# Strassen products for the merge gates and half of the branch gates of a two-layer encoder

## The chip, the cores and the metric

The kernel runs on one core of a Trainium2 chip. The metric is the device time of one execution in microseconds (us); below 0.2% (3.5 us) a difference can hardly be told from none.

## The reference, cut to what matters

```python
# x: (512, 1024) fp32, two layers, each:
h = rmsnorm(x, g_norm)
u = h @ w_in                       # one combined projection, all branches and gates
# A: 8 heads of differential attention -> o_a (rmsnorm over 128), B: dilated attention -> o_b,
# M: attention to 256 memory tokens -> o_m
y_a = (o_a * silu(dg)) @ w_br_diff     # dg, lg, mg: columns of u, 1024 + 512 + 512 wide
y_b = (o_b * silu(lg)) @ w_br_dil
y_m = (o_m * silu(mg)) @ w_br_mem
gates = sigmoid(mgate)                 # 3 x 1024 columns of u
merged = gates[0] * y_a + gates[1] * y_b + gates[2] * y_m
x = x + merged @ w_out
# end: rmsnorm(x, g_final)
```

## The kernel before, in words

The normalised input of a layer stands transposed in SBUF, as hT (128 x 8 x 512: eight k-slices of 128 channels, 512 tokens). Every fp32 operand is held as two parts: `split` (L95, L96) rounds a tile to its hi part on ScalarE (ACT) and subtracts that on VectorE (DVE) for the lo part, and `mm3` (L167 to L169) makes each product from three matmuls: hi by hi, hi by lo, lo by hi. A projection of 128 output channels (`proj_fm`) is so 8 x 3 = 24 matmuls on TensorE (PE) of 128x128 weights against 128x512 of hT. Weights come by DMA through `prefetch` (L141) two blocks ahead, in the order that `weight_order` writes out: 512 KB to `w_raw`, then `split` to `w_hi` and `w_lo` (128x1024 each).

A layer first does memory attention, then four rounds of differential and dilated attention. Work that PE can do at any time is woven with work that waits for softmaxes: `weave` takes turns between two generators. The last dilated attention, `dil_att(l, 3)`, has no partner. `diff_norm` makes the mean square of each head for the rmsnorm over 128 (`f_ms`), adds eps on ACT (`f_sq`, L446), takes the reciprocal on DVE (L447), and stores it to DRAM as `v_d`; the attention outputs go to DRAM as `u_d`. After this comes `merge`:

- 16 branch gates: `gate` makes x * sigmoid(x) of one projection; `u_raw` (a head's output, read back from `u_d`) is multiplied by it (L592), for the first eight also by the root of `v_d` (L589), and split to `u_hi`, `u_lo`, which stay in SBUF.
- For each of eight d (128 output channels): three merge gates (projections from hT, sigmoid), then the products `ya`, `yb`, `ym_ps` of the kept U with the branch weights, and their gated sum, split to `mg_hi`, `mg_lo`.

`out_proj` then multiplies these by `w_out`. The order of the instructions on each engine is set when the kernel is built, by a scheduler that runs a timeline of its own; on the chip each engine then takes its list in order.

Of the kernel before, what the change touches and what calls it, by code (L numbers as in the profile page):

```python
# [44 lines left out]
def encoder_kernel(ctx: ExitStack, tc: tile.TileContext, x, mem, g_norm, w_in, diff_lambda,  # L45
# [100 lines left out]
    ready = []  # L146

    def prefetch(n):
        while len(ready) < n and order:
            key, k, cols, pieces = order.pop(0)  # L150
            raw = wp.tile([128, k, cols], F32, tag="raw", name="w_raw", bufs=3)
            for k0, k1, c0, c1, src in pieces:
                dma(raw[:, k0:k1, c0:c1], src.rearrange("(k p) n -> p k n", p=128))
            hi = wp.tile([128, k, cols], F32R, tag="hi", name="w_hi", bufs=4)
            lo = wp.tile([128, k, cols], F32R, tag="lo", name="w_lo", bufs=3)
# [15 lines left out]
    def proj_fm(l, col):  # L171

        hi, lo = weight("in", l, col)
        o = mm([128, S])
# [4 lines left out]
    def gate(l, col):
# [397 lines left out]
        spill(o, 8 + h, P)  # L577


    def merge(l, yu, ym, lam_init):  # L580
        U = {}
        for i in U_ORDER:
            raw = yu.tile([128, S], F32, tag="ul", name="u_raw", bufs=3)
            dma(raw, u_d[i])
            if i < 8:
                v = yu.tile([128, S], F32, tag="uv", name="u_v", bufs=3)
# [10 lines left out]
        M = []  # L597
        for d in range(8):
            gs = []
            for b in range(3):  # L600
                o = proj_fm(l, MGATE + b * 1024 + d * 128)
                g = sg_tile(name="mgate")
                nc.scalar.activation(g, o, AF.Sigmoid)
                gs.append(g)
            whi, wlo = weight("ba", l, d)
            ya = mm([128, S])
            for k in range(8):
                mm3(ya, whi[:, k], wlo[:, k], U[k][0], U[k][1], k == 0, k == 7)
            whi, wlo = weight("bm", l, d)
            ym_ps = mm([128, S])  # L610
            yb = mm([128, S])
            for k in range(8):
                mm3(ym_ps if k < 4 else yb, whi[:, k], wlo[:, k], U[8 + k][0], U[8 + k][1], k % 4 == 0, k % 4 == 3)
            for g, y in zip(gs, (ya, yb, ym_ps)):
                nc.vector.tensor_tensor(out=g, in0=y, in1=g, op=ALU.mult)  # L615
            nc.vector.tensor_tensor(out=gs[0], in0=gs[0], in1=gs[1], op=ALU.add)
            nc.vector.tensor_tensor(out=gs[0], in0=gs[0], in1=gs[2], op=ALU.add)
            hi = ym.tile([128, S], F32R, tag="mg", name="mg_hi", bufs=16)
            lo = ym.tile([128, S], F32R, tag="mg", name="mg_lo", bufs=16)
            split(hi, lo, gs[0])  # L620
            M.append((hi, lo))
# [203 lines left out]
```

## Time and profile before

| | before |
|---|---|
| time, median of 3 runs | 1770.03 us (1769.4 to 1770.7) |
| the profiled execution: its time, its span | 1770.44 us, 1768.4 us |
| granted TensorE clock, mean | 0.998 |
| PE busy | 1743.8 us, 99% |
| DVE busy | 1005.5 us, 57% |
| ACT busy | 834.5 us, 47% |
| POOL (GpSimd) busy | 22.1 us, 1% |
| branch gates, first layer | about 540 to 637 us |
| merge gates and branch products, first layer | about 640 to 848 us |
| the same two in the second layer | about 1408 to 1505 us, 1505 to 1716 us |

A share is of the span, over stages with different limits. PE's busy time counts pipelined matmuls that overlap (a 128x512 matmul is shown with 0.39 us, but the next one starts 0.23 us after it), so the pitch, the distance from start to start, is what a matmul costs.

### The profile page before, as it was taken

How to read it: one execution, taken by the hardware profiler on the slowest of the kernel's cores; microseconds unless marked ns; L12 is line 12 of the kernel's file. 1: busy time of each engine (PE TensorE's matmuls, PEld its weight loads, DVE VectorE, ACT ScalarE, POOL GpSimd, SP SyncE). 2: the span in 40 equal slices, each digit the busy share in tenths (PEclk: the TensorE clock that was granted, in tenths of full speed). 3: DMA queues.
4: the chain of work that ended last, by engine and by line, in shares of the span. 5: the costliest groups of instructions: out<-in, count | busy, mean ns of one | idle time of the engine just before them, and what ended most of it. 6: DMA issues, size and time to landing. Idle time of an engine off the chain costs nothing.

```text
span 1768.4 us, 23429 instructions
## 1 busy us (share of the span) xinstructions
PE 1743.8 (99%) x9012; PEld 1496.0 (85%) x9012; DVE 1005.5 (57%) x1727; ACT 834.5 (47%) x1436; POOL 22.1 (1%) x45
## 2 busy tenths in 40 slices
PE   7999999999999999999999999999999999999998
PEld 6798889888888888888888898888988888888886
DVE  6566576666765663333465656658566747333333
ACT  6455555545555642222255555455454548322223
POOL 2200000000000000000000000000000000000000
PEclk9999999999999999999999999999999999999999
DMA  9643243332432643333572333324332336333342
GB/s 263 141 130 86 72 123 89 103 94 76 117 97 80 202 138 95 97 93 116 160 199 59 112 85 103 94 76 116 95 98 86 101 109 202 107 96 95 96 154 72
DMA packets 308847, 200.26 MB, mean 113 GB/s; under 512 B 14116, under 2 KB 283428, under 8 KB 308736
## 3 DMA queue, kind: packets, MB, share of 16 engines
q1 hardware_dynamic: 306704, 195.09, 38.3%
q0 software_dynamic: 2032, 3.68, 1.2%
q8 instruction: 71, 1.16, 0.3%
q14 instruction: 40, 0.33, 0.1%
HBM read 177.89 MB, written 20.83 MB: 112 GB/s over the span
## 4 chain that ended last, share of the span: by engine, by line
PE 97%; DMA 1%; ACT 1%; DVE 0%; issue 0%; SPq 0%; DVEq 0%; ACTq 0%
PE mm L167 27%; PE mm L169 27%; PE mm L168 27%; PE wT_ps L384 2%; PE f_s L407 2%; PE f_s L408 2%; DMA w_raw<-in_w_mem_kv 1%; PE f_o L168 1%; PE f_o L169 1%; PE f_o L167 1%; PE d_o L533 1%; PE d_s L509 1%; PE w_ps L522 0%; PE d_o L168 0%; PE d_o L169 0%; PE d_o L167 0%
## 5 line engine op out<-in xcount | busy, mean ns | idle before, releaser
L96 DVE TENSOR_TENSOR w_lo<-w_raw,w_hi 128x1024 fp32r<-128x1024 f32 (+2 forms) x296 | 335.8, 1135 | 436.1 <-PE mm L169 389.7
L95 ACT ACTIVATE w_hi<-w_raw 128x1024 fp32r<-128x1024 f32 (+2 forms) x296 | 293.3, 991 | 601.5 <-PE mm L168 296.0
L167 PE MATMUL mm<-hT_hi,w_hi 128*128 128x512 f32 x1344 | 529.9, 395 | 1.9 <-ACT hT_hi L95 1.9
L169 PE MATMUL mm<-hT_hi,w_lo 128*128 128x512 f32 x1344 | 527.3, 392 | 0.0
L168 PE MATMUL mm<-hT_lo,w_hi 128*128 128x512 f32 x1344 | 526.7, 392 | 0.0
L167 PEld LDWEIGHTS mm<-hT_hi,w_hi 128*128 128x128 f32 x1344 | 252.8, 188 | 53.2 <-ACT hT_hi L95 2.1
L169 PEld LDWEIGHTS mm<-hT_hi,w_lo 128*128 128x128 f32 x1344 | 252.9, 188 | 53.0 <-DVE w_lo L96 0.4
L168 PEld LDWEIGHTS mm<-hT_lo,w_hi 128*128 128x128 f32 x1344 | 253.0, 188 | 50.7
L169 PE MATMUL mm<-w_hi,hT_lo 128*128 128x384 f32 (+1 forms) x512 | 160.8, 315 | 0.0
L167 PE MATMUL mm<-w_hi,hT_hi 128*128 128x384 f32 (+1 forms) x512 | 160.0, 313 | 0.0
L168 PE MATMUL mm<-w_lo,hT_hi 128*128 128x384 f32 (+1 forms) x512 | 158.5, 310 | 0.0
L413 ACT ACTIVATE f_e<-f_e,f_st 128x512 f32<-128x512 f32 x128 | 91.9, 721 | 49.7 <-DVE f_st L410 49.7
L167 PE MATMUL mm<-u_hi,w_hi 128*128 128x512 f32 x256 | 101.2, 395 | 0.0
L169 PE MATMUL mm<-u_hi,w_lo 128*128 128x512 f32 x256 | 101.2, 395 | 0.0
L168 PE MATMUL mm<-u_lo,w_hi 128*128 128x512 f32 x256 | 101.1, 395 | 0.0
L167 PEld LDWEIGHTS mm<-w_hi,hT_hi 128*128 128x128 f32 x512 | 96.9, 189 | 1.0
L168 PEld LDWEIGHTS mm<-w_lo,hT_hi 128*128 128x128 f32 x512 | 96.8, 189 | 1.1
L169 PEld LDWEIGHTS mm<-w_hi,hT_lo 128*128 128x128 f32 x512 | 96.7, 189 | 0.0
L410 DVE CUSTOM_DVE_ANT_0 f_e<-f_s,f_bias 128x512 f32<-128x512 f32 x128 | 84.4, 681 | 6.8 <-PE f_s L408 6.7
L96 DVE TENSOR_TENSOR f_wTlo<-wT_ps,f_wThi 128x512 fp32r<-128x512 f32 x64 | 43.7, 683 | 31.4 <-ACT f_wThi L95 30.2
L615 DVE TENSOR_TENSOR mgate<-mm,mgate 128x512 f32<-128x512 f32 x48 | 33.0, 688 | 48.4 <-PE mm L169 48.4
L447 DVE RECIPROCAL f_sq<-f_sq 128x512 f32<-128x512 f32 x16 | 53.6, 3349 | 9.5 <-ACT f_sq L446 9.5
(203 smaller groups left out, 2403.9 us busy)
## 6 DMA issues: line engine op xcount, KB each, us to landing
w_raw<-in_w_in SPq DMA_DIRECT2D x168, 512.0 KB, 3.8
w_raw<-in_w_in SPq DMA_DIRECT2D x96, 128.0 KB, 2.4
w_raw<-in_w_mem_kv SPq DMA_DIRECT2D x16, 512.0 KB, 6.0
w_raw<-in_w_in SPq DMA_DIRECT2D x32, 256.0 KB, 2.9
u_raw<-u_d SPq DMA_DIRECT2D x32, 256.0 KB, 4.1
w_raw<-in_w_br_diff SPq DMA_DIRECT2D x16, 512.0 KB, 3.8
w_raw<-in_w_out SPq DMA_DIRECT2D x16, 512.0 KB, 3.9
f_bias<-tt_d SPq DMA_DIRECT2D x64, 112.0 KB, 4.1
```

The costliest lines, as they stand in the source:

```text
L95: nc.scalar.activation(hi, src, AF.Copy)
L96: nc.vector.tensor_tensor(out=lo, in0=src, in1=f32(hi), op=ALU.subtract)
L167: nc.tensor.matmul(o, lhsT=lh, rhs=rh, start=start, stop=False)
L168: nc.tensor.matmul(o, lhsT=lh, rhs=rl, start=False, stop=False)
L169: nc.tensor.matmul(o, lhsT=ll, rhs=rh, start=False, stop=stop)
L384: nc.tensor.transpose(t[:, i], s, ident)
L407: nc.tensor.matmul(sp, lhsT=qh[:, cs], rhs=K[s, m], start=True, stop=False)
L408: nc.tensor.matmul(sp, lhsT=ql[:, cs], rhs=K[s, m], start=False, stop=True)
L410: nc.vector.tensor_tensor_reduce(out=em.rearrange("p (c b) -> p c b", c=4), in0=sp, in1=bt[:, 3 - c:7 - c], op0=ALU.add, op1=ALU.min, scal ...
L413: nc.scalar.activation(em, em, AF.Exp, scale=-1.0, bias=stt[:, m:m + 1], accum_out=stt[:, 2 + m:3 + m])
L447: nc.vector.reciprocal(sq, sq)
L615: nc.vector.tensor_tensor(out=g, in0=y, in1=g, op=ALU.mult)
```

## The change

A pair of projections (two blocks of 128 columns) is one product of a 256x1024 weight block with the 1024x512 of hT. `pair` makes it by Strassen's scheme in Winograd's form: halves of the columns, of k and of the tokens, seven products instead of eight. Each product is 4 k-slices x 3 matmuls of 128x256. There are four branch pairs a layer (`U_PAIRS`, gates 4 to 7 and 12 to 15) and twelve merge pairs (`merge_steps`); eight branch gates stay single, and five of them (`gate_fill`) are now woven with `dil_att(l, 3)`. `load_pair` fetches the four quarters of a pair's weights (256 KB each) and makes the sums of quarters that the scheme needs with four GpSimd (POOL) operations; the sums are then split like other weights, in 3.5 units of 128x1024. `right_sums` makes the sums of hT's quarters once a layer: eight POOL additions of hi and lo (`b_q`), eight DVE subtractions, and eight splits into T0 to T3. Where a gate was one sigmoid and one multiply from PSUM, a pair is put together in SBUF by one ACT copy and eight DVE instructions of 128x256. The gated sums `m` are kept in fp32 (`m` tiles), and split into the place of hT after the last merge pair.

```diff
-U_ORDER = (8, 9, 10, 11, 0, 1, 2, 3, 4, 5, 12, 13, 14, 6, 7, 15)
+N_EARLY = 5
+U_ORDER = (8, 9, 10, 11, 0, 1, 2, 3)
+U_PAIRS = ((4, 12), (5, 13), (6, 14), (7, 15))
+def merge_steps(d0):
+    d1 = d0 + 1
+    return (("pair", (d0, 0), (d0, 1)), ("pair", (d0, 2), (d1, 2)), ("y", d0), ("pair", (d1, 0), (d1, 1)), ("y", d1))
...
+    def load_pair(key):
+        l, cols = key[1], key[2:]
+        pool = pair_pool[0]
+        t1, t2, t3 = [pool.tile([128, 8, 128], F32, tag="raw", name="s_raw", bufs=4) if i < 2 else
+                      wp.tile([128, 8, 128], F32, tag="raw", name="s_raw3", bufs=3) for i in range(3)]
+        t4 = pool.tile([128, 4, 128], F32, tag="raw4", name="s_raw4", bufs=2)
+        lo, up = slice(0, 4), slice(4, 8)
+        for t, part, f, k in ((t2, lo, 1, 0), (t3, up, 1, 1), (t1, lo, 0, 0), (t3, lo, 0, 1)):
+            src = w_in[l, k * 512:(k + 1) * 512, cols[f]:cols[f] + 128]
+            dma(t[:, part], src.rearrange("(k p) n -> p k n", p=128))
+        a11, a21, a12, a22 = t1[:, lo], t2[:, lo], t3[:, lo], t3[:, up]
+        tt = nc.gpsimd.tensor_tensor
+        tt(out=t2[:, up], in0=a21, in1=a22, op=ALU.add)
+        tt(out=t1[:, up], in0=t2[:, up], in1=a11, op=ALU.subtract)
+        tt(out=a21, in0=a11, in1=a21, op=ALU.subtract)
+        tt(out=t4, in0=a12, in1=t1[:, up], op=ALU.subtract)
...
+    def pair(l, colA, colB, B, gA, gB):
+        (b11, b21, b22), T = B
...
+        def prod(u, part, rhs):
...
+            o = mm([128, S], name="s_mm")[:, 0:256]
+            for k in range(4):
+                kk = 4 * part + k
+                mm3(o, hi[:, kk], lo[:, kk], rh[:, k], rl[:, k], k == 0, k == 3)
+            return o
...
+        nc.scalar.activation(c11, prod(0, 0, b11), AF.Copy)
+        add(c12, prod(0, 1, T[1]), c11)
+        add(c21, prod(1, 0, T[2]), c12)
+        o = prod(1, 1, T[0])
+        add(c22, o, c21)
+        add(c12, o, c12)
+        add(c11, prod(2, 0, b21), c11)
+        add(c21, prod(2, 1, T[3]), c21)
+        add(c12, prod(3, 0, b22), c12)
...
+    def right_sums(pool):
...
+                    b = pool.tile([128, 2, 256], F32, tag="uT", name="b_q", bufs=32)
+                    nc.gpsimd.tensor_tensor(out=b, in0=f32(hT_hi[:, ks, ts]), in1=f32(hT_lo[:, ks, ts]), op=ALU.add)
+                    q[kh, th] = b
...
+            sub(q[0, 0], q[0, 1], q[0, 0])
+            sub(q[0, 1], q[1, 1], q[0, 1])
+            sub(q[1, 1], q[1, 1], q[0, 0])
+            sub(q[1, 0], q[1, 0], q[1, 1])
+            ks = slice(2 * k2, 2 * k2 + 2)
+            for (hi, lo), b in zip(T, (q[0, 0], q[1, 1], q[0, 1], q[1, 0])):
+                split(hi[:, ks], lo[:, ks], b)
...
+        B = right_sums(yu)
+        for i in U_ORDER:
+            raw = load_u(i)
+            keep_u(i, raw, early[i] if i in early else gate(l, U_COLS[i]))
+        for two in U_PAIRS:
+            raws = [load_u(i) for i in two]
+            gs = [sg_tile(name="gate") for _ in two]
+            pair(l, *[U_COLS[i] for i in two], B, *gs)
+            for i, raw, g in zip(two, raws, gs):
+                sig = sg_tile(name="gate_s")
+                nc.scalar.activation(sig, g, AF.Sigmoid)
+                nc.gpsimd.tensor_tensor(out=raw, in0=raw, in1=g, op=ALU.mult)
+                keep_u(i, raw, sig)
...
+                    if step[1:] == LAST_PAIR:
+                        for e, m in enumerate(M):
+                            split(hT_hi[:, e], hT_lo[:, e], m)
...
-                weave((dil_att(l, j, P, dp), 4))
+                early = {}
+                def gate_fill():
+                    for i in U_ORDER[:N_EARLY]:
+                        early[i] = gate(l, U_COLS[i])
+                        yield
+                weave((gate_fill(), N_EARLY), (dil_att(l, j, P, dp), 4))
```

Places in the built order, first layer; a name's number tells one buffer from another, and the line numbers are each kernel's own.

On DVE before, where the first `u_raw` are kept, the work alternates between U tiles, gates and weights for single gates:

```order
L96 TENSOR_TENSOR w_lo_5665<-w_raw_5662,w_hi_5664 128x1024
L96 TENSOR_TENSOR w_lo_5710<-w_raw_5707,w_hi_5709 128x1024
L592 TENSOR_TENSOR u_raw_5357<-u_raw_5357,gate_5390 128x512
L592 TENSOR_TENSOR u_raw_5398<-u_raw_5398,gate_5431 128x512
L96 TENSOR_TENSOR u_lo_5395<-u_raw_5357,u_hi_5394 128x512
L184 TENSOR_TENSOR gate_5648<-mm_5623,gate_5648 128x512
L592 TENSOR_TENSOR u_raw_5439<-u_raw_5439,gate_5472 128x512
L96 TENSOR_TENSOR u_lo_5436<-u_raw_5398,u_hi_5435 128x512
L96 TENSOR_TENSOR w_lo_5755<-w_raw_5752,w_hi_5754 128x1024
L184 TENSOR_TENSOR gate_5693<-mm_5668,gate_5693 128x512
L96 TENSOR_TENSOR u_lo_5477<-u_raw_5439,u_hi_5476 128x512
L184 TENSOR_TENSOR gate_5738<-mm_5713,gate_5738 128x512
```

Each U tile is a multiply (L592) and a subtraction (L96) there, between those of gates and weights. On DVE of the change the same place begins with the reciprocal of the last `f_sq`, and the products of U, the subtractions for the sums of hT (`b_q`, T0 to T3) and the last single gates stand in one run:

```order
L548 RECIPROCAL f_sq_5506<-f_sq_5506 128x512
L698 TENSOR_TENSOR u_raw_5575<-u_raw_5575,gate_5241 128x512
L268 TENSOR_TENSOR b_q_5535<-b_q_5537,b_q_5535 128x512
L698 TENSOR_TENSOR u_raw_5582<-u_raw_5582,gate_5316 128x512
L107 TENSOR_TENSOR u_lo_5579<-u_raw_5575,u_hi_5578 128x512
L698 TENSOR_TENSOR u_raw_5589<-u_raw_5589,gate_5378 128x512
L285 TENSOR_TENSOR gate_5706<-mm_5681,gate_5706 128x512
L698 TENSOR_TENSOR u_raw_5596<-u_raw_5596,gate_5456 128x512
L107 TENSOR_TENSOR T0lo_5528<-b_q_5535,T0hi_5527 128x512
L107 TENSOR_TENSOR u_lo_5586<-u_raw_5582,u_hi_5585 128x512
L268 TENSOR_TENSOR b_q_5537<-b_q_5541,b_q_5537 128x512
L285 TENSOR_TENSOR gate_5761<-mm_5736,gate_5761 128x512
```

The subtractions for hT's sums and T0's lo part have come between the U tiles, and the reciprocal has come directly ahead of them. The end of that run, 43 instructions after the reciprocal, holds the lo parts of the first pair's weights (`w_lo_5721`, `w_lo_5780`) and the last halves of T3 and T1:

```order
L107 TENSOR_TENSOR w_lo_5721<-s_raw_5627,w_hi_5720 128x1024
L698 TENSOR_TENSOR u_raw_5714<-u_raw_5714,gate_5761 128x512
L268 TENSOR_TENSOR b_q_5559<-b_q_5559,b_q_5561 128x512
L107 TENSOR_TENSOR w_lo_5780<-s_raw3_5628,w_hi_5779 128x1024
L107 TENSOR_TENSOR T3lo_5534<-b_q_5539,T3hi_5533 128x512
L107 TENSOR_TENSOR T1lo_5530<-b_q_5561,T1hi_5529 128x512
L693 SCALAR_TENSOR_TENSOR u_raw_5922<-u_raw_5922,u_v_5924 128x512
L107 TENSOR_TENSOR u_lo_5711<-u_raw_5671,u_hi_5710 128x512
L107 TENSOR_TENSOR u_lo_5766<-u_raw_5714,u_hi_5765 128x512
L107 TENSOR_TENSOR T3lo_5534<-b_q_5559,T3hi_5533 128x512
L107 TENSOR_TENSOR w_lo_5812<-s_raw4_5629,w_hi_5811 128x512
L243 TENSOR_TENSOR gate_5777<-s_mm_5797,gate_5777 128x256
```

The second half of T3's lo part (`T3lo_5534<-b_q_5559`) has come last of these, behind U tiles that only the branch products read. On SP, the queue that issues the loads and stores, the stage before reads two `u_raw` ahead of the last store of a head:

```order
L153 DMA w_raw_5793<-in_w_in 128x8x128
L584 DMA u_raw_5357<-u_d_92 128x512
L584 DMA u_raw_5398<-u_d_92 128x512
L190 DMA u_d_92<-o_sb_5320 128x512
L584 DMA u_raw_5439<-u_d_92 128x512
L587 DMA u_v_5523<-v_d_93 128x512
L587 DMA u_v_5568<-v_d_93 128x512
L587 DMA u_v_5613<-v_d_93 128x512
```

The first two loads wait for no store of this stage there. In the change the loads of `u_raw` stand behind the two stores of `v_d`:

```order
L549 DMA v_d_93<-f_sq_5493 128x512
L291 DMA u_d_92<-o_sb_5422 128x512
L549 DMA v_d_93<-f_sq_5506 128x512
L688 DMA u_raw_5575<-u_d_92 128x512
L688 DMA u_raw_5582<-u_d_92 128x512
L688 DMA u_raw_5589<-u_d_92 128x512
L688 DMA u_raw_5596<-u_d_92 128x512
L688 DMA u_raw_5603<-u_d_92 128x512
L691 DMA u_v_5605<-v_d_93 128x512
L688 DMA u_raw_5614<-u_d_92 128x512
L691 DMA u_v_5616<-v_d_93 128x512
```

All loads of U tiles have moved behind the store of the last reciprocal, `f_sq_5506`. On PE of the change, the last single gate (`mm_5736`) ends and the first pair (`s_mm`) begins, two matmuls of each product first; before, single gates stood here:

```order
L216 MATMUL mm_5736<-hT_hi_88,w_hi_5622 128x512
L217 MATMUL mm_5736<-hT_lo_89,w_hi_5622 128x512
L218 MATMUL mm_5736<-hT_hi_88,w_lo_5623 128x512
L216 MATMUL s_mm_5783<-hT_hi_88,w_hi_5677 128x256
L217 MATMUL s_mm_5783<-hT_lo_89,w_hi_5677 128x256
L216 MATMUL s_mm_5797<-T1hi_5529,w_hi_5677 128x256
L217 MATMUL s_mm_5797<-T1lo_5530,w_hi_5677 128x256
L216 MATMUL s_mm_5815<-T2hi_5531,w_hi_5720 128x256
L217 MATMUL s_mm_5815<-T2lo_5532,w_hi_5720 128x256
L216 MATMUL s_mm_5829<-T0hi_5527,w_hi_5720 128x256
L217 MATMUL s_mm_5829<-T0lo_5528,w_hi_5720 128x256
L218 MATMUL s_mm_5783<-hT_hi_88,w_lo_5678 128x256
```

PE has come to the T tiles directly after the last single gate; behind 67 matmuls of the pair it needs the second half of `T3lo_5534`. Ahead of these rows, 41 matmuls of the last two single gates stand behind the last `f_ms`.

## Rows read from the trace of the kernel before

**Rows 1.** The page: busy time of PE, and the last chain by engine.

```profile
PE 1743.8 (99%) x9012; PEld 1496.0 (85%) x9012; DVE 1005.5 (57%) x1727; ACT 834.5 (47%) x1436; POOL 22.1 (1%) x45
...
PE 97%; DMA 1%; ACT 1%; DVE 0%; issue 0%; SPq 0%; DVEq 0%; ACTq 0%
```

**Rows 2.** Stretches of the first layer: length, busy time by engine, clock, DMA, GB/s.

```profile
540.00:584.00 44.00, 44.00 (x226) 37.03 (x225) 19.67 (x29) 20.51 (x28) 0.00 (x0) 1.00 0.32 97
584.00:600.00 16.00, 16.00 (x73) 13.23 (x73) 10.32 (x15) 13.73 (x18) 0.00 (x0) 1.00 0.84 265
600.00:640.00 40.00, 39.98 (x177) 32.79 (x176) 30.79 (x44) 27.37 (x37) 0.00 (x0) 1.00 0.58 172
640.00:850.00 210.00, 210.00 (x915) 171.43 (x914) 78.25 (x87) 59.09 (x75) 0.00 (x0) 1.00 0.36 105
```

**Rows 3.** PE's timeline, single gates: first and last of 49 matmuls in a row.

```profile
616.05 0.39 PE L167 MATMUL mm<-hT_hi,w_hi 128*128 128x512 f32 x1
...
626.93 0.39 PE L167 MATMUL mm<-hT_hi,w_hi 128*128 128x512 f32 x1
```

**Rows 4.** PE's timeline: first two and last of 51 matmuls of 128x256.

```profile
970.95 0.37 PE L168 MATMUL m_s<-mk_lo,m_qh 128*128 128x256 f32 x1
971.15 0.28 PE L169 MATMUL m_s<-mk_hi,m_ql 128*128 128x256 f32 x1
...
976.94 0.28 PE L168 MATMUL mm<-w_lo,hT_hi 128*128 128x256 f32 x1
```

**Rows 5.** Groups of instructions: weight loads, busy us, mean ns, idle before.

```profile
L167 PEld LDWEIGHTS mm<-hT_hi,w_hi 128*128 128x128 f32 x1344 | 252.8, 188 | 53.2 <-ACT hT_hi L95 2.1
```

**Rows 6.** ACT's timeline at the end of the last `diff_norm`: start, duration.

```profile
537.65 0.67 ACT L446 ACTIVATE f_sq<-f_ms,eps_t 128x512 f32<-128x512 f32 x1
```

**Rows 7.** DVE's timeline from there to the first kept U tiles.

```profile
538.86 3.34 DVE L447 RECIPROCAL f_sq<-f_sq 128x512 f32<-128x512 f32 x1
...
545.00 0.47 DVE L513 CUSTOM_DVE_ANT_0 d_e<-d_s,d_b,d_st 128x256 f32<-128x256 f32 x1
545.40 0.08 DVE L513 DVE_READ_ACCUMULATOR2_ANT d_st<- 128x1 f32 x1
...
588.04 0.69 DVE L592 TENSOR_TENSOR u_raw<-u_raw,gate 128x512 f32<-128x512 f32 x1 [1.06 <-DMA u_raw<-u_d]
588.65 0.68 DVE L96 TENSOR_TENSOR u_lo<-u_raw,u_hi 128x512 fp32r<-128x512 f32 x1
589.26 1.22 DVE L96 TENSOR_TENSOR w_lo<-w_raw,w_hi 128x1024 fp32r<-128x1024 f32 x1
590.39 0.68 DVE L184 TENSOR_TENSOR gate<-mm,gate 128x512 f32<-128x512 f32 x1
```

**Rows 8.** SP's timeline: the load behind the 588.04 row, and its store before.

```profile
584.87 0.32 SPq L190 DMA_DIRECT2D u_d<-o_sb  x1
585.24 0.43 SPq L584 DMA_DIRECT2D u_raw<-u_d  x1
```

**Rows 9.** DMA issues: count, KB each, median us from issue to landing.

```profile
w_raw<-in_w_in SPq DMA_DIRECT2D x32, 256.0 KB, 2.9
u_raw<-u_d SPq DMA_DIRECT2D x32, 256.0 KB, 4.1
```

**Rows 10.** Groups of DVE between 540 and 900 us: idle before, by releaser.

```profile
L96 DVE TENSOR_TENSOR u_lo<-u_raw,u_hi 128x512 fp32r<-128x512 f32 x16 | 11.0, 686 | 5.5 <-ACT u_hi L95 5.4
```

**Rows 11.** Stretch after PE's first wait, columns as in Rows 2.

```profile
48.00:52.00 4.00, 4.00 (x12) 3.10 (x12) 0.92 (x2) 0.00 (x0) 2.36 (x4) 0.57 0.79 155
```

**Rows 12.** PE's timeline in that stretch, two matmuls in a row.

```profile
50.18 0.63 PE L168 MATMUL mm<-hT_lo,w_hi 128*128 128x512 f32 x1
50.60 0.63 PE L169 MATMUL mm<-hT_hi,w_lo 128*128 128x512 f32 x1
```

**Rows 13.** Groups of POOL: busy us, mean ns.

```profile
masks.py:199 POOL TENSOR_SCALAR_AFFINE_SELECT ident<-ident 128x128 f32<-128x128 f32 x1 | 0.3, 312 | 0.1
...
L808 POOL MEMSET const-float32-1.0<- 128x1 f32 x1 | 0.1, 104 | 0.0
```

More of the change, by code (lines that the diff above doesn't have):

```diff
@@ L145, in encoder_kernel @@
     order = list(weight_order())
-    ready = []
-    def prefetch(n):
[L149 to L155, printed above, removed]
+    loaded, ready = [], []
@@ new lines, in encoder_kernel, with load @@
+    pair_pool = []
+    def load():
+        if order[0][0] == "pair":
+            load_pair(order.pop(0))
+            return
+        key, k, cols, pieces = order.pop(0)
+        raw = wp.tile([128, k, cols], F32, tag="raw", name="w_raw", bufs=3)
+        for k0, k1, c0, c1, src in pieces:
+            dma(raw[:, k0:k1, c0:c1], src.rearrange("(k p) n -> p k n", p=128))
+        loaded.append((key, raw))
+    def load_pair(key):
[14 more added lines that the diff above has]
+        tt(out=t4, in0=a12, in1=t1[:, up], op=ALU.subtract)
+        for i, t in enumerate((t1, t2, t3, t4)):
+            loaded.append((key + (i,), t))
@@ L156, in prefetch @@
+    def prefetch(n):
+        while len(ready) < n and (loaded or order):
+            if not loaded:
+                load()
+            key, raw = loaded.pop(0)
+            shape = list(raw.shape)
+            hi = wp.tile(shape, F32R, tag="hi", name="w_hi", bufs=4)
+            lo = wp.tile(shape, F32R, tag="lo", name="w_lo", bufs=3)
             split(hi, lo, raw)
             ready.append((key, hi, lo))
+        if pair_pool and len(loaded) < 3 and order and order[0][0] == "pair":
+            load()
@@ L577, in mem_att, with merge, load_u @@
         spill(o, 8 + h, P)
-    def merge(l, yu, ym, lam_init):
+    def merge(l, yu, ym, lam_init, early):
         U = {}
-        for i in U_ORDER:
-            raw = yu.tile([128, S], F32, tag="ul", name="u_raw", bufs=3)
+        pair_pool[:] = [yu]
+        m_tile = lambda name: ym.tile([128, S], F32, tag="m", name=name, bufs=8)
+        def load_u(i):
+            raw = m_tile("u_raw")
             dma(raw, u_d[i])
             if i < 8:
-                v = yu.tile([128, S], F32, tag="uv", name="u_v", bufs=3)
+                v = m_tile("u_v")
                 dma(v, v_d[i])
@@ L596, in merge @@
             U[i] = (hi, lo)
[L597 to L621, printed above, removed]
@@ new lines, in merge @@
+        M, G = [], {}
+        for d0 in range(0, 8, 2):
+            for step in merge_steps(d0):
+                if step[0] == "pair":
+                    gA, gB = [sg_tile(name="mgate") for _ in range(2)]
+                    pair(l, *[MGATE + b * 1024 + d * 128 for d, b in step[1:]], B, gA, gB)
+                    for g in (gA, gB):
+                        nc.scalar.activation(g, g, AF.Sigmoid)
+                    G[step[1]], G[step[2]] = gA, gB
+                    if step[1:] == LAST_PAIR:
+                        for e, m in enumerate(M):
+                            split(hT_hi[:, e], hT_lo[:, e], m)
+                    continue
+                d = step[1]
+                gs = [G.pop((d, b)) for b in range(3)]
+                whi, wlo = weight("ba", l, d)
+                ya = mm([128, S])
+                for k in range(8):
+                    mm3(ya, whi[:, k], wlo[:, k], U[k][0], U[k][1], k == 0, k == 7)
+                whi, wlo = weight("bm", l, d)
+                ym_ps = mm([128, S])
+                yb = mm([128, S])
+                for k in range(8):
+                    mm3(ym_ps if k < 4 else yb, whi[:, k], wlo[:, k], U[8 + k][0], U[8 + k][1], k % 4 == 0, k % 4 == 3)
+                for g, y in zip(gs, (ya, yb, ym_ps)):
+                    nc.vector.tensor_tensor(out=g, in0=y, in1=g, op=ALU.mult)
+                nc.vector.tensor_tensor(out=gs[0], in0=gs[0], in1=gs[1], op=ALU.add)
+                m = m_tile("m")
+                nc.vector.tensor_tensor(out=m, in0=gs[0], in1=gs[2], op=ALU.add)
+                M.append(m)
+                if d == 7:
+                    split(hT_hi[:, d], hT_lo[:, d], m)
@@ L625, in out_proj @@
+        pair_pool[:] = []
+    def out_proj(l, done):
         for n in range(2):
@@ L701, in done @@
                 ns = slice(n * 512, (n + 1) * 512)
-                xr = ym.tile([128, 512], F32, tag="xr", name="xr", bufs=2)
+                xr = ym.tile([128, 512], F32, tag="m", name="xr", bufs=8)
                 dma(xr, x_v[c][:, ns])
@@ L705, in done @@
                 dma(x1_d[c][:, ns], xt[c][:, ns])
-            out_proj(l - 1, M, done)
+            out_proj(l - 1, done)
             close(ym_c)
@@ L739, in encoder_kernel @@
         ym_c, ym = opened(f"ym{l}", "right")
-        M = merge(l, yu, ym, lam_init)
+        merge(l, yu, ym, lam_init, early)
         close(yu_c)
@@ L769, in done @@
         dma(out_v[c][:, h1], y[:, h1])
-    out_proj(DEPTH - 1, M, done)
+    out_proj(DEPTH - 1, done)
     close(ym_c)
```

49 lines of the change are left out of this document (36 added, 13 removed).

## The prediction, made before the changed kernel ran

> **What bounds the kernel now.** I read the page first: PE is busy for 99% of the span, and 97% of the chain that ended last is PE's [rows 1]. Then the stretches of the stage that is changed: from 540 to 850 us PE has no gap worth the name, while DVE is busy for 19.7 of 44.0 us at the end of the attention, for 41.1 of 56.0 while the branch gates are made, and for 78.3 of 210.0 after them [rows 2]. So a matmul that is removed shows in full wherever the other engines keep up, and between 584 and 640 us, DVE has little room left. PE's timeline then gives what a matmul costs: 48 steps of 128x512 from 616.05 to 626.93 us are 0.2267 us each [rows 3]. For 128x256, 50 steps from 970.95 to 976.94 us are 0.120 each, or 0.118 without the first, which stands before a longer one [rows 4]. A weight load takes 0.188 us [rows 5], more than either half-size step, so loads overlap in that run already.
>
> **The saving.** A pair of projections was 2 x 24 = 48 matmuls of 128x512, 48 x 0.2267 = 10.88 us. It becomes 7 x 12 = 84 of 128x256, 84 x 0.120 = 10.08 us. That is 0.80 us a pair; with 16 pairs a layer and two layers, 32 x 0.80 = 25.6 us. At 0.118 it would be 32 x 0.97 = 31.0 us. I take 0.120: the run it comes from mixes operands as a pair does.
>
> **The entry to the first pair.** PE meets T0 to T3 for the first time here. I count from the moment at which PE has made the last `f_ms`, and call it the mark. Behind it PE has 41 matmuls of the last two single gates, 41 x 0.2267 = 9.3 us, and 67 of the first pair, 67 x 0.120 = 8.0 us, before it needs the second half of T3's lo part: 17.3 us of cover. On the other side a chain runs:
>
> - ACT's scaling of `f_sq` takes 0.67 us [rows 6] and the reciprocal 3.34 us [rows 7]: 4.0 us, and with hand-offs 4.1.
> - SP then issues the store of `v_d`, and only behind it the first load of `u_raw`. A store's issue took 0.4 us (584.87 to 585.24), and the load issued at 585.24 us [rows 8] let DVE go at 588.04 [rows 7], 2.8 us later; the median landing is 4.1 us [rows 9]. Between these I take 3.5. So the first U tile can be multiplied at 4.1 + 0.4 + 3.5 = 8.0 us.
> - Behind the reciprocal, DVE has 43 instructions up to that half of T3: 40 of 128x512 at 0.605 us from start to start (588.04 to 588.65, and to 589.26), and three splits of 128x1024 at 1.13 (589.26 to 590.39) [rows 7]. That is 27.6 us, to 35.6.
> - 13 of them subtract a hi part that ACT makes just before. The `u_lo` group idled 5.5 us over 16 such hand-offs, 0.34 each [rows 10]: 4.4 us, to 40.0.
>
> PE so waits 40.0 - 17.3 = 22.7 us. No edit hides this: all other PE work of the layer is listed behind. After a wait the granted clock fell before: from 48 to 52 us it was 0.57, the lower of its two levels [rows 11], with a step of 0.42 us [rows 12] in place of 0.227; some eight such steps are 1.7 us more. Together 24.4 us a layer.
>
> **The other branch pairs.** From there to the last part of the first merge pair's weights, DVE has 59 instructions: 12 of 128x1024, 19 of 128x512 and 28 adds of 128x256, for which I take 0.40 us by the nearest row (545.00 to 545.40) [rows 7]. 13.6 + 11.5 + 11.2 = 36.3 us, with 21 hand-offs at 0.34 43.4 us. PE has 17 + 3 x 84 + 72 = 341 matmuls, 40.9 us. DVE ends 2.5 us later; PE pays that too. A layer then loses 26.9 us, two 53.8. The second layer's lists have the same order. Lower bound, if hand-offs overlap and the load lands in 2.8: (34.9 - 17.3) + 0 = 17.6 us a layer, 35 for both. Upper, with 4.1 us landing: 0.6 more a layer.
>
> **What I cost at nothing.** The merge pairs add DVE work, but there it has room: of 210 us it was busy for 78 [rows 2], and per two d it would be 3 x (3.5 x 1.13 + 8 x 0.40) + 4 x 1.13 + 10 x 0.605 = 32 us, of PE's 3 x 10.08 + 96 x 0.2267 = 52. The pair sums on POOL have no price in this trace. From below, DVE's 0.61 us for the same shape; from above, four times the 0.312 us that a 128x128 select took, 1.25; the slope from a 128x1 memset at 0.104 to that select [rows 13] gives 0.104 + 4 x 0.208 = 0.94, which I take. Four of them, 3.8 us, with the 256 KB loads (2.9 us [rows 9]) and the splits, are done two pairs (20 us) ahead. Without that cover, each pair would wait some 2.9 + 3.8 = 6.7 us. The splits of `m` into hT's place, seven of 0.61 us on DVE, lie under the last 48 branch matmuls (10.9 us). The five gates beside `dil_att(l, 3)` are as many PE matmuls as before, earlier; if the attention's last steps are then short of PE work, up to one gate's 5.4 us is missing, which I leave to the range.
>
> **Sum.** 1768.4 - 25.6 + 53.8 = 1796.6 us of span. The profiled execution's time was 2.0 us over its span, and 0.4 above the median, so 1.6 is added: 1798 us.
>
> **Rivals.** *POOL holds DVE up.* At the entry and in the branch pairs, POOL's operations run beside DVE's, nearly all of which read two tiles in SBUF. If one stops the other for its whole length: of the 16 operations at the entry the first eight (8 x 0.94 = 7.5 us) fall before the first load lands, the others add 7.5 us; in the branch pairs 20 operations (18.8 us) fall on 59 DVE instructions of which the 28 adds, 11.2 us, read PSUM, so some 7.6 us more. 15 us a layer, 30 in all: 1828 us. With POOL at 0.61 it is 4.9 + 1.0 a layer, 1810 us; at 1.25, where the first eight end 2.0 late, 2.0 + 10.0 + 13.8, 1850. Nothing in the trace of before speaks for or against it, since POOL is idle after the start [rows 2]. The Trainium skill states this rule, in "SBUF — State Buffer", section "Who interferes with whom": a VectorE instruction with two SBUF inputs contends with a GpSimd instruction that reads SBUF, and the one that comes second is blocked for the other's whole length; no run here shows it so far. Of POOL's price the skill has a figure in "GPSIMD Engine Reference", section 3.1, "Elementwise — side-by-side cycle accounting": 4497 ns for an fp32 addition of 2048 columns, by which I estimate 1.12 us for 512; this rival would then give 1840 us.
>
> *The wait is only that of the chain that the products need (the other side).* If the U tiles were done by the mark, 16 instructions of T and sums (9.7 us), three weight splits (3.4) and one more (0.6), 13.7 us, would lie behind 8.0 us: a wait of 8.0 + 13.7 - 17.3 = 4.4, with the clock 6.1 us a layer, and nothing in the later pairs. 1768.4 - 25.6 + 12.2 + 1.6 = 1757 us, faster. It decides below 12.8 us of loss a layer. Against it speaks the built order: about 25 instructions on U tiles stand ahead of T3's last half, behind loads that stand behind the reciprocal's store.
>
> *Half-size matmuls are held up by weight loads.* At 10.88/84 = 0.1295 us a step the saving is gone: 1798 + 25.6 = 1824 us. The run of [rows 4] speaks against it.
>
> *A wait of about 13 us a layer,* from shorter hand-offs and earlier loads, would make it even: 1770 us, no change.
>
> **Chances.** The forecast, 1780 to 1812 us: 0.47. POOL holding DVE up, 1812 to 1838: 0.25. The short wait: 0.14, below 1766. Between 1766 and 1780: 0.10, half of it within 0.2% (3.5 us, about what can be told from no change). Half-size steps held up, or something not thought of: 0.04. Left outside the range are the short wait and what may lie above 1838: 1766 to 1838. The forecast's own range is 1780 to 1812. Faster 0.14, the same 0.05, slower 0.81.
>
> **What would show it.** The steps of `s_mm` at 0.12 us, the first pair of each layer waiting for a T tile's lo part on DVE, once some 23 us in all, and DVE without a gap before it; the first `u_raw` load issued directly behind the `v_d` store. DVE instructions that take longer while POOL runs would show the first rival. The prediction is wrong if DVE reaches T3 before PE does, or if the pairs between the entry and `out_proj` wait for sums of weights.

## The result, and the profile after

The changed kernel takes 1826.88 us, the median of 4 runs (1824.3 to 1827.95), against 1769.72 for the one before: a ratio of 1.0321, interval 1.0306 to 1.0337. It is 57 us slower; I had forecast 28, at 1798 us. The profiled execution has a span of 1824.3 us.

The page of the changed kernel, busy time and the last chain, beside [rows 1]: PE is busy for 15 us less, POOL for 288 us more, and 8% of the chain is now DVE's.

```profile
PE 1728.9 (95%) x10164; PEld 1538.4 (84%) x10164; DVE 1227.2 (67%) x2031; ACT 892.6 (49%) x1536; POOL 310.4 (17%) x205
...
PE 86%; DVE 8%; DMA 2%; issue 2%; POOL 1%; ACT 1%; SPq 0%; DVEq 0%; POOLq 0%; ACTq 0%
```

Stretches of its first layer, columns as in [rows 2]. The single gates end at 583 us, the first products of U begin at 686. Between these DVE is busy throughout, PE is not, and the granted clock falls to 0.70 where PE works in pieces. Behind 680 us PE is full again.

```profile
560.00:580.00 20.00, 18.62 (x96) 15.49 (x95) 10.37 (x7) 5.35 (x10) 7.10 (x6) 1.00 0.23 73
580.00:600.00 20.00, 3.26 (x15) 2.37 (x13) 19.10 (x18) 9.23 (x15) 15.16 (x11) 0.70 0.74 230
600.00:620.00 20.00, 11.67 (x67) 10.45 (x68) 20.00 (x29) 11.37 (x17) 9.10 (x3) 0.71 0.52 151
620.00:640.00 20.00, 16.37 (x131) 15.62 (x131) 19.79 (x24) 10.29 (x14) 19.72 (x11) 1.00 0.35 100
640.00:660.00 20.00, 15.82 (x115) 15.32 (x114) 20.00 (x21) 9.47 (x14) 14.43 (x9) 0.83 0.32 93
660.00:680.00 20.00, 17.85 (x146) 17.19 (x145) 19.89 (x29) 11.15 (x18) 9.50 (x5) 1.00 0.24 68
680.00:700.00 20.00, 20.00 (x125) 17.80 (x124) 13.18 (x17) 6.73 (x9) 7.73 (x4) 1.00 0.40 117
```

DVE's timeline of the changed kernel at the entry, beside [rows 7]. The mark (the last `f_ms`) is at 573.0 us. The same kinds of instruction that take 0.68 us at 583.82 take 1.75 from 590.31 on, and 0.68 again from 602.00.

```profile
574.31 3.35 DVE L548 RECIPROCAL f_sq<-f_sq 128x512 f32<-128x512 f32 x1 [3.26 <-ACT f_sq L547]
580.90 1.30 DVE L698 TENSOR_TENSOR u_raw<-u_raw,gate 128x512 f32<-128x512 f32 x1 [3.24 <-DMA u_raw<-u_d]
582.12 1.78 DVE L268 TENSOR_TENSOR b_q<-b_q 128x512 f32<-128x512 f32 x1
583.82 0.68 DVE L698 TENSOR_TENSOR u_raw<-u_raw,gate 128x512 f32<-128x512 f32 x1
...
593.65 1.74 DVE L268 TENSOR_TENSOR b_q<-b_q 128x512 f32<-128x512 f32 x1
595.31 1.75 DVE L693 SCALAR_TENSOR_TENSOR u_raw<-u_raw,u_v 128x512 f32<-128x512 f32 x1
596.99 1.75 DVE L268 TENSOR_TENSOR b_q<-b_q 128x512 f32<-128x512 f32 x1
598.66 1.75 DVE L107 TENSOR_TENSOR T2lo<-b_q,T2hi 128x512 fp32r<-128x512 f32 x1
...
602.00 0.68 DVE L268 TENSOR_TENSOR b_q<-b_q 128x512 f32<-128x512 f32 x1
...
617.45 0.68 DVE L107 TENSOR_TENSOR T3lo<-b_q,T3hi 128x512 fp32r<-128x512 f32 x1
```

POOL's timeline over the same time. Its sums of weights start at 593.14, 594.80, 596.48 and 598.15, DVE's instructions at 593.65, 595.31, 596.99 and 598.66: both go in steps of 1.67 us, one of the one and one of the other.

```profile
572.90 10.45 POOL L266 TENSOR_TENSOR b_q<-hT_hi,hT_lo 128x512 f32<-128x512 f32 x8 [492.64 <-PE d_o L218]
...
593.14 1.70 POOL L190 TENSOR_TENSOR s_raw<-s_raw 128x512 f32<-128x512 f32 x1
594.80 1.71 POOL L189 TENSOR_TENSOR s_raw<-s_raw 128x512 f32<-128x512 f32 x1
596.48 1.71 POOL L190 TENSOR_TENSOR s_raw<-s_raw 128x512 f32<-128x512 f32 x1
598.15 3.38 POOL L191 TENSOR_TENSOR s_raw<-s_raw,s_raw 128x512 f32<-128x512 f32 x2
```

The first row is eight additions for hT. Shown in two parts, the first seven, beside which DVE ran nothing but the reciprocal, took 8.75 us, 1.25 each; the eighth, beside DVE's first multiply, took 1.75. The reciprocal, which reads one tile, ran its usual 3.3 us beside them.

```profile
572.90 8.75 POOL L266 TENSOR_TENSOR b_q<-hT_hi,hT_lo 128x512 f32<-128x512 f32 x7 [492.64 <-PE d_o L218]
...
581.61 1.75 POOL L266 TENSOR_TENSOR b_q<-hT_hi,hT_lo 128x512 f32<-128x512 f32 x1
```

DVE's groups between 540 and 900 us before, and between 540 and 920 us after (mean ns behind the comma). Splits of 128x1024 take 1494 ns for 1222 before, the pairs' multiplies by a gate 1279 for 686. The adds of 128x256, which take one operand from PSUM, take 411 here and 414 in e3 below, where POOL reads no weights. There are 28 of them in four pairs: seven a pair, not the eight of the section on the change.

```profile
L96 DVE TENSOR_TENSOR w_lo<-w_raw,w_hi 128x1024 fp32r<-128x1024 f32 x64 | 78.0, 1222 | 126.2 <-PE mm L169 115.3 <-issue 7.7 <-PE mm L168 3.0
...
L592 DVE TENSOR_TENSOR u_raw<-u_raw,gate 128x512 f32<-128x512 f32 x16 | 10.9, 686 | 1.2 <-DMA u_raw<-u_d 1.1
```

```profile
L107 DVE TENSOR_TENSOR w_lo<-s_raw,w_hi 128x1024 fp32r<-128x1024 f32 x48 | 71.7, 1494 | 16.8 <-issue 16.8
...
L243 DVE TENSOR_TENSOR gate<-s_mm,gate 128x256 f32<-128x256 f32 x28 | 10.8, 411 | 0.2
L698 DVE TENSOR_TENSOR u_raw<-u_raw,gate_s 128x512 f32<-128x512 f32 x8 | 10.2, 1279 | 0.0
```

PE's timeline: the first pair, behind a wait, its first matmul with T3, and the first and last of 168 half-size matmuls of the merge stage, 167 steps of 0.1187 us.

```profile
603.74 0.58 PE L216 MATMUL s_mm<-hT_hi,w_hi 128*128 128x256 f32 x1 [20.48 <-ACT w_hi L106]
...
619.12 0.39 PE L216 MATMUL s_mm<-T3hi,w_hi 128*128 128x256 f32 x1 [2.31 <-DVE gate L243]
...
718.64 0.28 PE L216 MATMUL s_mm<-hT_hi,w_hi 128*128 128x256 f32 x1
...
738.46 0.28 PE L218 MATMUL s_mm<-hT_hi,w_lo 128*128 128x256 f32 x1
```

The wait of 20.48 us ends with the hi part of the pair's weights on ACT. On ACT's list that stands directly behind a `u_hi`, which waited for DVE's multiply at 600.33 us; POOL's eight sums had ended by 601.53. So DVE's run is behind this wait too, and not a sum that came late.

```profile
602.11 0.63 ACT L106 ACTIVATE u_hi<-u_raw 128x512 fp32r<-128x512 f32 x1 [2.19 <-DVE u_raw L698]
602.65 1.04 ACT L106 ACTIVATE w_hi<-s_raw 128x1024 fp32r<-128x1024 f32 x1
```

**An account of the stage.** From the mark to the first product of U, PE has work for 41 x 0.2267 + 6 x 84 x 0.1187 = 69.1 us. It took 113.2 in the first layer and 115.5 in the second. The table has this time in the first layer, beside PE's work in it (matmuls counted, at 0.2267 and 0.1187 us), and splits it by DVE's timeline: the instructions at the time they take while POOL is idle (0.607 us for 128x512, 1.137 for 128x1024, 0.335 for an add of 128x256; the reciprocal 3.3), the time by which they were longer, and the rest, nearly all of it idle time of DVE.

| kernel | mark to first U product | PE's work | DVE's own | longer by | rest |
|---|---|---|---|---|---|
| the change | 113.2 | 69.1 | 78.6 | 29.3 | 5.3 |
| e1, no sums of weights | 96.2 | 69.1 | 78.6 | 9.2 | 8.4 |
| e3, POOL only writes | 96.0 | 69.1 | 78.6 | 6.4 | 11.0 |
| e2, sums on DVE | 106.7 | 69.1 | 98.4 | 1.7 | 6.6 |
| e7, U tiles later | 117.6 | 69.1 | 79.2 | 26.5 | 11.9 |
| e8, the same without sums of weights | 97.4 | 69.1 | 79.2 | 7.2 | 11.0 |
| e11, U loads by ACT's queue | 115.3 | 69.1 | 78.6 | 30.1 | 6.6 |
| e12, two branch pairs | 99.4 | 70.9 | 71.7 | 21.5 | 6.2 |
| e4, merge pairs only | 81.7 | 72.8 | 66.0 | 10.2 | 5.5 |
| e9, pairs from d = 2, gates early | 69.9 | 69.1 | 57.0 | 1.7 | 11.2 |

PE's loss of 44.1 us in the change is so 9.5 us of DVE's own work above PE's, 29.3 by which DVE's instructions were longer, and 5.3 of rest. The clock that fell is no further cause here: DVE has 0.3 us of idle time in all between 580.9 and 680 us, so PE's slower steps lay under waits for it. With 29.1 us saved, the two layers' losses make 90.5 - 29.1 = 61.4 us, and the span rose by 55.9; the other 5.5 us, gained outside these stages, are not assigned.

### The profile page after: what moved, and what is told of

It reads as the page before. It is cut to its first block, busy times and chain, and to the rows that moved or that the text cites. A ratio compares the mean times of both kernels' runs of the same rounds, so it can differ in the third digit from the quotient of the medians.

```text
span 1824.3 us, 26859 instructions
## 1 busy us (share of the span) xinstructions
PE 1728.9 (95%) x10164; PEld 1538.4 (84%) x10164; DVE 1227.2 (67%) x2031; ACT 892.6 (49%) x1536; POOL 310.4 (17%) x205
## 4 chain that ended last, share of the span: by engine, by line
PE 86%; DVE 8%; DMA 2%; issue 2%; POOL 1%; ACT 1%; SPq 0%; DVEq 0%; POOLq 0%; ACTq 0%
PE mm L216 20%; PE mm L218 20%; PE mm L217 20%; PE s_mm L216 4%; PE s_mm L218 4%; PE s_mm L217 4%; DVE w_lo L107 3%; PE wT_ps L485 2%; PE f_s L508 2%; PE f_s L509 2%; DVE u_raw L698 1%; DMA w_raw<-in_w_mem_kv 1%; DVE u_lo L107 1%; DVE b_q L268 1%; PE f_o L216 1%
## 5 line engine op out<-in xcount | busy, mean ns | idle before, releaser
L216 PE MATMUL mm<-hT_hi,w_hi 128*128 128x512 f32 x832 | 330.2, 397 | 2.5 <-ACT hT_hi L106 2.5
L217 PE MATMUL mm<-hT_lo,w_hi 128*128 128x512 f32 x832 | 327.7, 394 | 0.0
L218 PE MATMUL mm<-hT_hi,w_lo 128*128 128x512 f32 x832 | 327.2, 393 | 0.0
L106 ACT ACTIVATE w_hi<-s_raw 128x1024 fp32r<-128x1024 f32 (+1 forms) x128 | 120.9, 948 | 183.8 <-PE mm L217 100.6
L218 PE MATMUL mm<-w_hi,hT_lo 128*128 128x384 f32 (+2 forms) x640 | 209.9, 329 | 0.0
L216 PE MATMUL mm<-w_hi,hT_hi 128*128 128x384 f32 (+2 forms) x640 | 209.5, 328 | 0.0
L217 PE MATMUL mm<-w_lo,hT_hi 128*128 128x384 f32 (+2 forms) x640 | 208.2, 326 | 0.0
L107 DVE TENSOR_TENSOR w_lo<-s_raw,w_hi 128x1024 fp32r<-128x1024 f32 (+1 forms) x128 | 168.7, 1319 | 33.7 <-issue 33.7
L216 PE MATMUL s_mm<-hT_hi,w_hi 128*128 128x256 f32 x384 | 113.0, 294 | 45.8 <-ACT w_hi L106 39.0
L218 PE MATMUL s_mm<-hT_hi,w_lo 128*128 128x256 f32 x384 | 111.7, 291 | 3.3 <-DVE w_lo L107 3.3
```

Of the source, the lines that this page charges most:

```text
L106: nc.scalar.activation(hi, src, AF.Copy)
L107: nc.vector.tensor_tensor(out=lo, in0=src, in1=f32(hi), op=ALU.subtract)
L216: nc.tensor.matmul(o, lhsT=lh, rhs=rh, start=start, stop=False)
L217: nc.tensor.matmul(o, lhsT=lh, rhs=rl, start=False, stop=False)
L218: nc.tensor.matmul(o, lhsT=ll, rhs=rh, start=False, stop=stop)
```

## The experiments

Theory 1: POOL's and DVE's instructions that read two tiles in SBUF hold each other up, and DVE, which is full from the mark to the first U product, passes this on to PE. Theory 2: the loss is the order at the entry (U loads behind a store, U tiles ahead of T), and DVE's longer instructions only fill time that it would have waited.

**e1**, the sums of weights left out:

```diff
-        tt(out=t2[:, up], in0=a21, in1=a22, op=ALU.add)
...
+        for t, f, k in ((t2[:, up], 1, 1), (t1[:, up], 0, 1), (t4, 0, 0)):
+            s = w_in[l, k * 512:(k + 1) * 512, cols[f]:cols[f] + 128]
+            dma(t, s.rearrange("(k p) n -> p k n", p=128))
```

> Leaves out the sums of the pairs' weights: the three tiles that POOL made are loaded by three more DMAs of 256 KB instead, so the products are of other numbers. POOL keeps the eight sums for hT and the multiplies of the branch pairs. Theory 1 (POOL's and DVE's instructions with two SBUF operands take turns, and this costs the loss beyond my forecast): DVE's stretched instructions between 580 and 680 us return to 0.61 and 1.14 us except beside the few POOL operations left; a layer loses about 20 us at the entry and 2 behind it, 1785 to 1798 us. Theory 2 (the order at the entry alone: loads behind the store of v_d, and DVE's long run): no change, 1820 to 1830.

Measured: 1789.41 us (1788.68 to 1790.35), ratio 1.0107, interval 1.0092 to 1.0122. As theory 1 has it: 37 of the 57 us are gone, although three more loads a pair were made.

**e3**, POOL writes at the same places and reads nothing there:

```diff
-        tt(out=t2[:, up], in0=a21, in1=a22, op=ALU.add)
...
+        for o in (t2[:, up], t1[:, up], a21, t4):
+            for _ in range(2):
+                nc.gpsimd.memset(o, 0.5)
```

> Leaves out the sums of the pairs' weights: at each of their places POOL does two memsets of the same tile, which read nothing from SBUF, so the products are of other numbers. POOL stays busy at the same places. If only reads of POOL stand against DVE's second SBUF operand: as without the sums, 1785 to 1798 us, DVE at 0.61 and 1.14 us beside the memsets. If any work of POOL on SBUF does it: near the change, 1815 to 1830. Theory 2: also near the change.

Measured: 1787.46 us (1786.29 to 1787.85), ratio 1.0095, interval 1.0079 to 1.011. Its groups between 540 and 920 us on DVE, and POOL's memsets in the whole run: 132 us of POOL's writes leave DVE's splits at 1215 ns.

```profile
L107 DVE TENSOR_TENSOR w_lo<-s_raw,w_hi 128x1024 fp32r<-128x1024 f32 x48 | 58.3, 1215 | 28.5 <-issue 28.5
```

```profile
L189 POOL MEMSET s_raw<- 128x512 f32 x256 | 131.7, 527 | 297.9 <-DVE w_lo L107 212.3 <-DMA s_raw<-in_w_in 71.6 <-ACT u_hi L106 7.8
```

So it is not POOL's being busy that costs, but its reading. Two memsets are 1.05 us, a sum 1.25, so the pairs' weights were also ready a little sooner. That this matters is not seen: e1, where POOL spends no time at all on these weights, is 2 us slower than e3, and in the change DVE, which PE waits for, has next to no idle time in which it could wait for a sum.

**e2**, the sums on DVE:

```diff
-        tt = nc.gpsimd.tensor_tensor
+        tt = nc.vector.tensor_tensor
...
-                nc.gpsimd.tensor_tensor(out=raw, in0=raw, in1=g, op=ALU.mult)
+                nc.vector.tensor_tensor(out=raw, in0=raw, in1=g, op=ALU.mult)
```

> The whole computation; the sums of the pairs' weights and the multiplies of the branch pairs are made on DVE in place of POOL, which keeps only the eight sums for hT. Theory 1: DVE gets 24 instructions of 0.61 us more in the branch pairs of a layer (14.5 us), and loses the 22 to 30 us by which POOL stretched its own: faster than the change, 1790 to 1805 us. Theory 2, or POOL as a free helper: DVE, which is full there, gets 29 us more in the two layers, 1850 us or more.

Measured: 1811.14 us (1809.44 to 1812.85), ratio 1.0226. Faster than the change by 16 us, though DVE, the full engine, does all the work that POOL did; less fast than I expected, since I counted 24 further instructions in the stage and 35 fell into it (27 sums, some for the first merge pairs, and 8 multiplies); DVE's own time rose by 19.8 us.

**e7 and e8**, the first eight U tiles behind the first branch pair; e8 without the sums of weights, as e1:

```diff
-        for i in U_ORDER:
-            raw = load_u(i)
-            keep_u(i, raw, early[i] if i in early else gate(l, U_COLS[i]))
+        late = {i: early[i] if i in early else gate(l, U_COLS[i], ut("gate")) for i in U_ORDER}
...
             pair(l, *[U_COLS[i] for i in two], B, *gs)
+            for i in U_ORDER:
+                if i in late:
+                    keep_u(i, load_u(i), late.pop(i))
```

> The whole computation of the change; the first eight U tiles are multiplied and split behind the first branch pair, not ahead of it. DVE's run from the last reciprocal to the last half of T3 falls from 43 to 31 instructions, 7.3 us of its own. Theory 1 (DVE is full to the end of the branch pairs, by POOL): the entry's wait falls by 7 to 12 us a layer, and most is lost again behind it: 1810 to 1827. Theory 2 (the entry's order alone): 2 x 12 us gained or more, 1800 or less.

> The same order, and the sums of the pairs' weights left out (loaded by DMA in their place, the products are of other numbers). Without them the change took 1789 us, with about 21 us a layer lost in the branch stage. The entry should wait 7 us less, and DVE has 41.8 us of work, and some 8 us of POOL's multiplies beside it, against PE's 40.9 behind it, so 1 to 9 are lost there: 1775 to 1787.

Measured: e7 1831.72 us (1829.92 to 1832.33), ratio 1.0342; e8 1791.02 (1788.56 to 1792.44), ratio 1.0109. Neither gained; both miss, e7 by 5 us beyond its range, e8 by 4. With the sums left out the single wait at the entry falls (4.97 us before the first `s_mm`, 8.02 in e1), but what was moved is waited for behind the first pair: the stage took 97.4 us, and 96.2 in e1. Theory 2 falls: the order within the stage, as changed here and in e11, moves the wait and does not shorten it. Why e7 was 5 us slower than the change is open; the table has it in the rest.

**e11**, U loads by another queue:

```diff
-            dma(raw, u_d[i])
+            (nc.scalar.dma_start if i in U_ORDER[:5] else dma)(raw, u_d[i])
```

> The whole computation of the change; ACT's queue issues the loads of the first five u_raw, so they no longer stand behind SP's store of the last reciprocal. DVE's run then starts some 3.2 us earlier in each layer (it stood idle from 577.7 to 580.9 us). If DVE is what PE waits for from there to the end of the branch pairs, all of it is gained: 1820 us, 1816 to 1823. If not: 1825 to 1829.

Measured: 1827.32 us (1826.35 to 1829.2), ratio 1.0322: no gain, against what I took to follow from theory 1; the value is in the range that I gave to the other side. DVE's U tiles start at 579.00 us, 1.9 earlier, but run into POOL's additions for hT, which now take 11.77 us for 10.45. The table has 30.1 us of longer instructions for 29.3, and a stage 2.1 us longer. Why none of the earlier start was left was not separated.

**e12**, two branch pairs a layer:

```diff
-U_PAIRS = ((4, 12), (5, 13), (6, 14), (7, 15))
+U_PAIRS = ((6, 14), (7, 15))
```

> The whole computation of the change with two branch pairs a layer in place of four; four more gates are single. By an account of DVE's work from the last f_ms to the first branch products: two pairs fewer take 2 x (3.5 x 1.14 + 8 x 0.335 - 3.5 + 6 x 1.07 of POOL's hold) = 19 us from DVE, and give PE 1.6 more: a layer loses 22 us there in place of 42.5. 1791 us, 1785 to 1797. If the loss is that of entering the pairs at all: 1815 or more.

Measured: 1798.96 us (1794.83 to 1799.23), ratio 1.0155: 28 us gained, 2 less than the range allowed. PE's loss in the stage is 99.4 - 70.9 = 28.5 us, for 44.1. The loss goes with the amount of DVE work in the stage, POOL's hold on it included, not with entering the pairs.

**e4, e5, e6, e9 and e10**, fewer pairs. In all five the branch gates are single; e5, e9 and e10 have pairs from d = 2 on; e5 and e6 drop the gates set early beside `dil_att(l, 3)`; e10 makes the sums on DVE. What was expected follows in the order of the table.

```diff
-U_PAIRS = ((4, 12), (5, 13), (6, 14), (7, 15))
+U_PAIRS = ()
...
+    if d0 < FIRST_D:
+        return tuple(("one", (d0, b)) for b in range(3)) + (("y", d0),) + tuple(("one", (d1, b)) for b in range(3)) + (("y", d1),)
```

> The whole computation; the sixteen branch gates are single as before, the twelve merge pairs of a layer stay as in the change, with all their POOL sums. Both theories put the loss between the last single gate and the first branch products: it should go, since sixteen single gates now cover the sums of hT. 24 pairs x 0.80 us are saved: 1750 us, 1747 to 1760. If half-size products or their sums cost something of their own in the merge stage, 1770 or more.

> The whole computation; branch gates single and woven as in the kernel before (no gates set beside the last dilated attention by hand), merge gates of d = 0 and 1 single, and pairs from d = 2 on, nine a layer. The six further single gates, 33 us of PE, cover the sums of hT and of the first pairs' weights: no wait should be left, and 18 x 0.80 = 14.4 us are saved: 1756 us, 1753 to 1760. If DVE, stretched by POOL, holds PE up in the merge stage too, 1765 or more.

> The whole computation; as the run with merge pairs only, but the last dilated attention is left without the five gates set beside it, as in the kernel before. There PE lost some 8 us a layer in the first merge pairs and 4 in that attention. If the weaving costs those 4: 1757 us, 1754 to 1761. If it costs nothing and only the first pairs do: 1765.

> The whole computation; merge pairs from d = 2 on, and the five gates set beside the last dilated attention as in the change. Without them PE lost 6.1 us a layer where the first U tiles are kept (590 to 610 us) and 1.9 in that attention; with them the run of merge pairs only lost 4.3 in that attention and nothing behind it. So 2 x 3.7 us less than 1759.4: 1752 us, 1748 to 1757. If the gates' place does not matter: 1759.

> As the run with merge pairs from d = 2 on and the gates set early, with the sums of weights on DVE in place of POOL. If POOL's hold on DVE costs nothing where DVE has room: the same within 3 us. If it costs PE time in the merge stage too: faster by more than 3 us.

| kernel | median us | ratio to before | interval |
|---|---|---|---|
| e4 | 1764.80 | 0.997 | 0.9959 to 0.998 |
| e5 | 1759.37 | 0.9937 | 0.9925 to 0.995 |
| e6 | 1773.56 | 1.0015 | 1.0006 to 1.0024 |
| e9 | 1750.88 | 0.9892 | 0.9875 to 0.9908 |
| e10 | 1751.24 | 0.9889 | 0.9874 to 0.9904 |

e4 missed by 15 us: with all merge pairs the first of them still come while DVE is full (76.2 of 81.7 us in the table). e6 missed to the other side: without the early gates DVE falls behind, and PE waits for a gate (2.9 us) where single gates still run. e5 and e9 came as expected, and e9 beats both kernels: 19 us faster than before. The early gates are worth 8.5 us between e5 and e9, and 8.8 between e6 and e4. The merge stage of e9, 700 to 860 us, columns as in [rows 2], and DVE's splits in it: POOL is busy for 46.9 us, the splits are longer there as well (1408 ns), but DVE has room and PE is full. e10, where POOL does nothing in that stage, takes the same time.

```profile
700.00:860.00 160.00, 160.00 (x989) 143.26 (x988) 105.58 (x147) 62.10 (x83) 46.94 (x27) 1.00 0.39 122
```

```profile
L110 DVE TENSOR_TENSOR w_lo<-s_raw,w_hi 128x1024 fp32r<-128x1024 f32 x21 | 29.6, 1408 | 11.7 <-issue 11.7
```

## Why the prediction was right and where it was wrong

**The direction and the places were right, the size was half, and the direction in part by luck.** A layer was to lose 26.9 us between the mark and the branch products; it lost 113.2 - 69.1 = 44.1 in the first and 46.4 in the second. Of the 26.9, the 4.4 us of hand-offs, the 1.7 of clock and the 2.5 behind the entry, itself made of hand-offs, did not occur as such. Without them the forecast's own terms come to 35.6 - 17.3 = 18.3 us a layer, 1768.4 - 25.6 + 36.6 + 1.6 = 1781 us, or 1777.5 with the saving as measured. That it was so clearly slower came from POOL's hold, which the forecast had at nothing.

- *The saving*: a pair costs 84 x 0.1187 = 9.97 us, so 0.91 is saved, not 0.80; 29 us in all, near the end that I named and did not take. Half-size matmuls were not held up by weight loads.
- *The first load*: DVE could go 7.9 us behind the mark; forecast 8.0.
- *DVE's run to T3*: it ended 45.0 us behind the mark, not 40.0. My 27.6 us of own time were right. The 4.4 us of hand-offs were not there: DVE has no idle time in that run. About 9.6 us of longer instructions were there in their place (1.22, 1.70 and 1.08 us, and seven of 1.67, for 0.61 each). The sign that I named, one wait of some 23 us for T3's lo part, did not come as such: PE stood for 20.48 us before the first matmul of the pair, held by the same run of DVE through ACT, and, after two waits of about 1 us, for 2.31 us before T3. The slow steps, 0.21 us for 0.12, lay ahead of that second wait, so my 1.7 us for the clock did not add to it.
- *The other branch pairs*: from T3 on PE has 437 matmuls, 51.9 us, and took 68.2: 16 us late for a forecast of 2.5. That is the term that failed. I had costed POOL's sums at nothing, hidden two pairs ahead. When they were ready did not decide; what they do to DVE did: 29.3 us of longer instructions in the stage, of which the run to T3 has 9.6 and this part the rest.
- *POOL's price*: 1.25 us alone, at my upper bound and well above the 0.94 that I took.
- *The merge stage and the splits into hT's place*: no loss, as said; from the first to the last U product 189.1 us for 8 x 48 x 0.2334 + 10 x 9.97 = 189.3 of work, with U products at 0.2334 us from start to start before and after.

**The rival that decided** was POOL holding DVE up, to which I gave 0.25, and whose 1828 us is within 1.2 of the result. It is not a confirmed sum, though. It put 15 us a layer on top of 11.5 us of hand-offs that did not occur; the hold was 29 us a layer. The Trainium skill's rule on which instructions meet ("SBUF — State Buffer", "Who interferes with whom") agrees with each row here: two SBUF operands against a POOL read are slowed (1494 ns for 1222), one from PSUM is not (411), POOL's writes alone are not felt (1215). By the same rule of the Trainium skill the second is held for the other's whole length; here the measurement differs, since the two take 1.25 + 0.61 = 1.86 us one after the other, and went at 1.67 a pair. The Trainium skill's figure for POOL ("GPSIMD Engine Reference", section 3.1), by which I estimated 1.12 us, is below the 1.25 measured.

What the runs show: 37 of the 57 us go with the reads of POOL's weight sums (e1, e3). In the other 20, POOL's hold by its multiplies and hT's sums still has a part (9.2 us a layer of longer instructions in e1). What is left of e1's loss, 9.5 us a layer of DVE's own work above PE's and 8.4 of rest, is not far above the 14.6 that a layer saves. The loss comes with the amount of DVE work put into a stage in which DVE had little room (e12, e4, e9), not with its order (e7, e8). Single terms below 5 us, as in e11, stay open.

## What to carry to other kernels

Before giving work to an idle engine, ask what it shares with the full one: here POOL's 34 sums and multiplies of a layer's stage cost DVE more (29.3 - 1.7 = 27.6 us) than doing them itself (19.8 us). For a stage in which an engine is already busy for 41 of 56 us, add up that engine's whole work, with what the other engines' reads add to it, against the bound engine's, from the point at which it starts to the point at which all is needed, rather than following one chain. A trade of matmuls for vector work pays where vector work has room: with eighteen of the thirty-two pairs, placed behind enough single gates, the kernel was 19 us faster; with all of them 57 slower. Of the 19, 18 x 0.91 = 16.4 are the matmuls; the early gates may have given the rest, but without pairs they were not run.

## What the runs showed of the hardware

DVE and POOL, both reading two tiles of 128x512, went in lock step, one instruction each per 1.67 us, where DVE alone takes 0.61 and POOL alone 1.25. POOL's memsets of the same tiles (0.53 us) were not felt by DVE. A 128x256 matmul stepped at 0.1187 us over 168 in a row, each with a weight load of 0.19 us beside it.
